# Hybrid attention and SSM layer: where 26 conditioning granules are summed, and in which order the middle stage loads

## The chip, the cores and the metric

The kernel runs on one core of a Trainium2 chip. The metric is the device time of one launch in microseconds (us). The engines are TensorE (PE, matrix multiply), VectorE (DVE), ScalarE (ACT), GpSimd (POOL) and SyncE (SP, which here issues the large transfers). The core has 16 DMA engines between HBM and the on-chip memory.

## The reference, cut to what matters

One decoder layer on 256 tokens of width 2048, all in float32. A vector `c` gives six vectors of 2048 numbers (shift, scale and gate of both sub-layers) through one large matrix, `w_ada`, of 2048 by 12288 (100 MB):

```python
c_act = jax.nn.silu(c)
ada = c_act @ w_ada[l] + b_ada[l]
sh_m, sc_m, gt_m, sh_f, sc_f, gt_f = [t[:, None, :] for t in jnp.split(ada, 6, axis=-1)]

h = rmsnorm(x, g_pre_mix[l]) * (1.0 + sc_m) + sh_m
proj = h @ w_in[l]                       # q (1024), k, v (128 each), u (1024)
attn = sliding_window_attention(q, k, v, attn_sinks[l])   # window 128, 16 heads
y = s5_ssm(u, ...)                       # 64 groups of 16 channels, 64 complex states each
z = gelu(y);  ssm = z * sigmoid(z @ w_glu[l])
merged = concat([rmsnorm(attn, g_attn_out[l]), rmsnorm(ssm, g_ssm_out[l])])
x = x + (1.0 + gt_m) * rmsnorm(merged @ w_out[l], g_post_mix[l])

h = rmsnorm(x, g_pre_ffn[l]) * (1.0 + sc_f) + sh_f
up = causal_depthwise_conv(h @ w_up[l], conv_w[l], conv_b[l])
ff = gelu(gate) * val @ w_down[l]
x = x + (1.0 + gt_f) * rmsnorm(ff, g_post_ffn[l])
```

## The kernel before, in words

**Granules.** Each of the six vectors is made in 16 granules of 128 numbers; a granule needs a block of `w_ada` of 1 MB. There are two ways. VectorE sums it (`ada_sum`, L142): one instruction multiplies the 128x2048 block by the broadcast `silu(c)` and adds along the row. Or PE does it (`ada_mm`, L155, 32 matmuls for a granule; ScalarE copies the result; `ada_cols`, L162, two small matmuls turn it into a column). `ON_PE` says which granules are PE's: ten of the first gate (GT_M), all of the FFN shift (SH_F), all of the first shift, four of the first scale (SC_M 0, 1, 11, 12). The rest of GT_M and the FFN scale SC_F, 22 granules, are the list `late_ada`: VectorE sums them in the middle stage, the GLU and the output projection.

**Stages in time.** Projection A (to about 160 us) makes q, k, v, u column by column; between its granules VectorE and GpSimd make Z, the complex tables of the SSM, in eight chunks (`z_chunk`). The middle stage (to 260 us) holds the rest of the input projection (`B(k4, kk)`, `mm_winb`, four loads `winb`), the attention of eight head pairs (`att_scores`, `att_max`, `att_norm`, `pv`, `att_out`) and the SSM: `k_half` makes kernel values in `kdz` and writes them out to a DRAM buffer `md`; `toeplitz` (L741) reads `md` back as the matrix `M` in four loads; `scan` runs 13 recurrence steps on VectorE; `y_mu` (L813) multiplies by `M`, `y_cx` (L826) by Z. Each group of four matmuls of `y_mu` uses two of `M`'s four loads, and its first eight groups use all four. Then GLU (`ps_g` L1039), the output projection (`wout` loads, split by `out_hl` into a high and a low part by ScalarE and VectorE, matmuls to `mix` at L566 and L557, to 385 us), the up projection (`ps_u` L1261, L1263), the down projection. In the first 16 tiles of the up projection, SH_F is made by PE in eight pairs (`shift_pair`, `shift_cols`).

**Order.** PE and SP run in the order in which the code is written, everywhere. In the middle stage VectorE, ScalarE and GpSimd do too: `in_order` (L72) records each of their instructions behind the one before, which is why their rows there show L72. So the code's order is the queue order, and an instruction that waits holds all behind it on its engine. All 1 MB loads (`raw`, L96) go through one pool of six buffers; a load waits until the buffer that it takes has been read. Which load is issued when is set by the list `loads` and by `pump(n)`, which takes the next n letters: w is a `winb`, d a granule that VectorE will sum, p one for a PE pair, g a part of `w_glu`. `do()` sums the oldest loaded d granule on VectorE and pumps one; `pair()` has PE multiply two p granules and pumps two; `cols()` finishes the oldest pair:

```python
def cols():
    res, part, o = pairs.pop(0)
    ada_cols(part, 2, res)
    A.copy(ada[:, o:o + 2], res)
```

In the output projection, step k loads `wout` ahead, calls `ld` once or twice (one `late_ada` load each), runs its matmuls and sums one or two granules.

## Time and profile before

| what | value |
|---|---|
| device time, median of 3 runs | 1172.07 us (1169.95 to 1172.98) |
| the profiled execution's own time | 1171.59 us |
| its span in the trace | 1169.8 us |
| mean granted TensorE clock | 0.987 of full speed |
| PE busy | 1126.6 us, 96% |
| VectorE busy | 873.7 us, 75% |
| ScalarE busy | 556.4 us, 48% |
| DMA | 325.87 MB, 279 GB/s on average |

Busy shares are averages over stages with different limits, so they don't say what a change in one stage is worth; that is read from the stage's own windows and waits. The program's time is 1.8 us more than the span.

### The profile page before, as it was taken

How to read it: one execution, taken by the hardware profiler on the slowest of the kernel's cores; microseconds unless marked ns; L12 is line 12 of the kernel's file. 1: busy time of each engine (PE TensorE's matmuls, PEld its weight loads, DVE VectorE, ACT ScalarE, POOL GpSimd, SP SyncE). 2: the span in 40 equal slices, each digit the busy share in tenths (PEclk: the TensorE clock that was granted, in tenths of full speed). 3: DMA queues.
4: the chain of work that ended last, by engine and by line, in shares of the span. 5: the costliest groups of instructions: out<-in, count | busy, mean ns of one | idle time of the engine just before them, and what ended most of it. 6: DMA issues, size and time to landing. Idle time of an engine off the chain costs nothing.

```text
span 1169.8 us, 18819 instructions
## 1 busy us (share of the span) xinstructions
PE 1126.6 (96%) x7504; PEld 944.9 (81%) x7504; DVE 873.7 (75%) x1369; ACT 556.4 (48%) x943; POOL 103.4 (9%) x96
## 2 busy tenths in 40 slices
PE   7899998989998999999999999999999999999996
PEld 5788876768786888888888888888888788888885
DVE  5987938636789787568999989886766776776555
ACT  3122143563534464446665665655555544444443
POOL 6005801024000200000000000000000000000002
PEclk9999998999998999999999999999999999999998
DMA  9899987787999469885787787865555777777712
GB/s 385 345 362 361 353 286 289 277 328 283 347 357 414 156 252 356 333 326 216 290 294 278 294 290 268 301 256 184 198 194 180 272 273 296 279 282 286 260 66 73
DMA packets 49144, 325.87 MB, mean 279 GB/s; under 512 B 5520, under 2 KB 7744, under 8 KB 12448
## 3 DMA queue, kind: packets, MB, share of 16 engines
q1 hardware_dynamic: 48240, 321.06, 73.6%
q0 software_dynamic: 672, 3.55, 0.8%
q8 instruction: 59, 0.97, 0.3%
q14 instruction: 29, 0.24, 0.1%
q10 hardware_dynamic: 144, 0.05, 0.0%
HBM read 317.27 MB, written 7.37 MB: 278 GB/s over the span
## 4 chain that ended last, share of the span: by engine, by line
PE 63%; issue 22%; DVE 8%; ACT 3%; DMA 2%; POOL 1%; DVEq 0%; ACTq 0%; POOLq 0%
PE ps_u L1261 27%; PE ps_u L1263 14%; PE accA L337 7%; PE ps_ada L155 4%; DVE l_wout L72 2%; PE ps_g L1039 2%; DVE ada L142 2%; PE accB L607 2%; DMA wout<-in_w_out_dram 1%; DVE scn L72 1%; PE ps_u L1250 1%; PE mix L557 1%; DMA shm<-in_w_ada_dram 1%; PE ps_wt L298 1%; PE ps_y L813 1%
## 5 line engine op out<-in xcount | busy, mean ns | idle before, releaser
L547 ACT CAST h_wup<-wup 128x1024 fp32r<-128x1024 f32 x168 | 176.5, 1052 | 194.6 <-PE ps_u L1261 175.6
L548 DVE TENSOR_TENSOR l_wup<-wup,h_wup 128x1024 fp32r<-128x1024 f32 x168 | 205.3, 1223 | 84.3 <-ACT h_wup L547 77.0
L1261 PE MATMUL ps_u<-h2B,h_wup 128*128 128x512 f32 x688 | 243.7, 395 | 0.0
L1261 PE MATMUL ps_u<-h2A,h_wup 128*128 128x512 f32 x688 | 243.5, 395 | 0.0
L1263 PE MATMUL ps_u<-h2A,l_wup 128*128 128x256 f32 x688 | 191.9, 279 | 0.0
L1263 PE MATMUL ps_u<-h2B,l_wup 128*128 128x256 f32 x688 | 191.5, 278 | 0.0
L548 DVE TENSOR_TENSOR l_wdn<-wdn,h_wdn 128x1024 fp32r<-128x1024 f32 x88 | 107.6, 1224 | 66.0 <-ACT h_wdn L547 65.9
L1261 PEld LDWEIGHTS ps_u<-h2B,h_wup 128*128 128x128 f32 x688 | 129.0, 188 | 30.3 <-issue 0.6
L1261 PEld LDWEIGHTS ps_u<-h2A,h_wup 128*128 128x128 f32 x688 | 128.9, 188 | 29.8 <-issue 0.4
L1263 PEld LDWEIGHTS ps_u<-h2A,l_wup 128*128 128x128 f32 x688 | 129.4, 188 | 0.8 <-issue 0.6
L547 ACT CAST h_wdn<-wdn 128x1024 fp32r<-128x1024 f32 x88 | 92.6, 1053 | 78.6 <-PE dn L566 70.4
L1263 PEld LDWEIGHTS ps_u<-h2B,l_wup 128*128 128x128 f32 x688 | 129.4, 188 | 0.2 <-issue 0.2
L337 PE MATMUL accA<-hT,win 128*128 128x256 f32 x448 | 109.6, 392 | 1.6 <-ACT hT L397 1.6
L566 PE MATMUL dn<-h_wdn,fl 128*128 128x512 f32 x336 | 105.0, 396 | 1.4 <-DVE fl L548 1.4
L566 PE MATMUL dn<-h_wdn,fh 128*128 128x512 f32 x336 | 106.0, 396 | 0.0
L566 PE MATMUL dn<-l_wdn,fh 128*128 128x512 f32 x336 | 106.0, 395 | 0.0
L337 PEld LDWEIGHTS accA<-hT,win 128*128 128x128 f32 x448 | 83.0, 194 | 14.7 <-issue 3.4
L142 DVE CUSTOM_DVE_ANT_0 ada<-ada,cbc 128x2048 f32<-128x2048 f32 x38 | 86.6, 2284 | 0.0
L566 PEld LDWEIGHTS dn<-h_wdn,fl 128*128 128x128 f32 x336 | 63.0, 188 | 17.1 <-DVE fl L548 1.9
L566 PEld LDWEIGHTS dn<-l_wdn,fh 128*128 128x128 f32 x336 | 63.1, 188 | 15.2
L566 PEld LDWEIGHTS dn<-h_wdn,fh 128*128 128x128 f32 x336 | 63.0, 188 | 15.2
L1417 DVE CUSTOM_DVE_ANT_0 wupt<-wupt,shbc 128x2048 f32<-128x2048 f32 x22 | 50.3, 2284 | 0.2 <-DMA wupt<-in_w_up_t_dram 0.2
(357 smaller groups left out, 1568.0 us busy)
## 6 DMA issues: line engine op xcount, KB each, us to landing
wup<-in_w_up_dram SPq DMA_DIRECT2D x88, 1024.0 KB
ada<-in_w_ada_dram SPq DMA_DIRECT2D x64, 1024.0 KB
wdn<-in_w_down_dram SPq DMA_DIRECT2D x44, 1024.0 KB
wupt<-in_w_up_t_dram SPq DMA_DIRECT2D x22, 1024.0 KB
scm<-in_w_ada_dram SPq DMA_DIRECT2D x16, 1024.0 KB
shm<-in_w_ada_dram SPq DMA_DIRECT2D x16, 1024.0 KB
wout<-in_w_out_dram SPq DMA_DIRECT2D x16, 1024.0 KB
win<-in_w_in_a_dram SPq DMA_DIRECT2D x16, 896.0 KB
```

What stands on the lines that cost most here:

```text
L72: self.last = self.no_earlier(getattr(self.e, name)(*args, **kw))
L142: return nc.vector.tensor_tensor_reduce(t, t, cbc, 1.0, 0.0, ALU.mult, ALU.add, accum_out=dst)
L155: PE.matmul(ps[32 * j:32 * j + 32, v * P:(v + 1) * P], lhsT=csil[:, kc:kc + 1].to_broadcast([P, 32]), rhs=t[:, kc * P:(kc + 1) * P], start ...
L337: PE.matmul(accA[ct // 2][:, (ct % 2) * S:(ct % 2 + 1) * S], lhsT=winA[k][:, ct * P:(ct + 1) * P], rhs=hk, start=(k == 0 and ct % 2 == 0), ...
L547: (A.copy if e[0] == "a" else V.tensor_copy)(hi, src)
L548: (V if e[1] == "v" else G).tensor_sub(lo, src, hi.bitcast(F32))
L566: PE.matmul(acc[tt * 4 + half * 2 + n2], lhsT=a_[:, tk], rhs=b_[:, n2 * 512:(n2 + 1) * 512], start=(kk == 0 and first), stop=(kk == nk - 1 ...
L607: PE.matmul(accB[ct // 2][:, (ct % 2) * S:(ct % 2 + 1) * S], lhsT=wt[:, kk * 512 + ct * P:kk * 512 + (ct + 1) * P], rhs=hT[k // 8][:, k % ...
L1039: PE.matmul(psg[ct][:, :S], lhsT=wg_[ct // 2][:, (ct % 2 * 8 + k) * P:(ct % 2 * 8 + k + 1) * P], rhs=zf[:, k], start=(k == 0), stop=(k == 7))
L1261: PE.matmul(ps, lhsT=wh[:, ks], rhs=h2[kk // 4][:, kk % 4].rearrange("p a b -> p (a b)"), start=(kk == 0), stop=(kk == KD - 1), skip_group ...
L1263: PE.matmul(ps[:, :S], lhsT=wl[:, ks], rhs=h2_of(kk)[0], start=False, stop=(kk == KD - 1), skip_group_check=True)
L1417: V.tensor_tensor_reduce(t, t, shbc[0], 1.0, 0.0, ALU.mult, ALU.add, accum_out=rlate[:, vg, f:f + 1])
```

## The change

The diff makes these edits. (1) Four granules of the FFN shift, SH_F 0 to 3, leave PE: `late_ada` grows from 22 to 26, and `shift_pair` runs for six pairs in place of eight; one small VectorE add puts the bias on the four columns. SC_M 10 is made on PE and SC_M 12 by VectorE. (2) VectorE makes six chunks of Z in place of five, GpSimd two in place of three, with its own scratch tile. (3) In the middle stage five sums by VectorE are added in front (`do()` twice, `do(0)` three times), the load list begins in another order and has 15 d in place of 10, and more of it is pumped ahead of `md` and of `M`. (4) `att_max(2)` and `att_norm(2)` come one and two scan steps earlier. (5) `cols()` copies its result on VectorE, not ScalarE, and `pv(5)`, `pv(6)` stand ahead of `z_part(0)`, `z_part(1)`. (6) The output projection loads and sums one granule fewer (11 in place of 12).

```diff
-Z_AT = (10, 11, 12, 13, 14)
-
-ON_PE = {(v, m) for v, n in ((SH_M, KD), (GT_M, 10), (SH_F, KD)) for m in range(n)} | {(SC_M, m) for m in (0, 1, 11, 12)}
+Z_AT = (10, 11, 12, 13, 14, 15)
+
+NSH = 4
+ON_PE = {(v, m) for v, n in ((SH_M, 0), (GT_M, 0), (SH_F, NSH)) for m in range(n, 10 if v == GT_M else KD)} | {(SC_M, m) for m in (0, 1, 10, 11)}
...
-    Z_AT_G = (10, 11, 12)
+    Z_AT_G = (10, 11)
...
-    late_ada = [(v, m) for v in (GT_M, SC_F) for m in range(KD) if (v, m) not in ON_PE]
+    late_ada = [(v, m) for v in (GT_M, SC_F, SH_F) for m in range(KD) if (v, m) not in ON_PE]
...
-    loads = "w w w w d p p d p p d p p d p p d p p d g d g d g d g d".split()
+    loads = "d d w d d w d w w d p p d p p d p p d p p d p p d g d g d g d g d".split()
...
             if n in Z_AT:
-                z_chunk(Z_AT.index(n), V, ztmp2)
+                z_chunk((0, 1, 2, 3, 6, 7)[Z_AT.index(n)], V, ztmp2)
...
-    def do():
+    def do(n=1):
         after[0].no_earlier(ada_sum(*ada_in.pop(0), cbc[0]))
-        pump()
+        pump(n)
...
         ada_cols(part, 2, res)
-        A.copy(ada[:, o:o + 2], res)
+        V.tensor_copy(ada[:, o:o + 2], res)
...
+    do()
     k_half(0)
+    do()
     att_scores(0)
     k_half(1)
     att_max(0)
+    do(0)
     v_tok()
...
     att_max(1)
+    do(0)
+    do(0)
     B(0, 2)
...
     B(0, 3)
-    pump()
+    pump(3)
...
     B(1, 1)
-    scan(2)
+    scan(1)
     att_max(2)
     att_out(1)
     B(1, 2, 3)
-    pump()
-    scan(2)
+    pump(2)
+    scan(1)
     att_norm(2)
     B(2, 0)
+    scan(2)
     pv(2)
...
     pair()
+    pv(5)
     z_part(0)
-    pv(5)
     cols()
...
-            ld(2 if k in (4, 6, 8) else 1)
+            ld(2 if k in (4, 6) else 1)
...
-        for _ in range(2 if k in (5, 7, 9) else 1):
+        for _ in range(2 if k in (5, 7) else 1):
...
+    V.tensor_add(shift[:, 1, :NSH], ada[:, SH_F * KD:SH_F * KD + NSH], col("bT")[:, SH_F * KD:SH_F * KD + NSH])
...
-                if n % 2 == 0 and n < KD:
-                    shp = shift_pair(n)
-                elif n < KD:
+                if n % 2 == 0 and n < KD - NSH:
+                    shp = shift_pair(NSH + n)
+                elif n < KD - NSH:
```

SP's queue around `md` and `M`, before (`winb` is a w load, `ada` a d load, `ud` and `U` carry u through DRAM):

```order
L619 DMA ud<-uT 128x8x128 x2
L637 DMA U<-ud 128x1024 x2
L664 DMA md<-kdz 8x16x1024 x8
L96 DMA ada_56_1565<-in_w_ada_dram 128x2048
L741 DMA M<-md 128x2048 x4
```

The same place now:

```order
L622 DMA ud<-uT 128x8x128 x2
L640 DMA U<-ud 128x1024 x2
L97 DMA ada_56_1332<-in_w_ada_dram 128x2048
L97 DMA winb_1371<-in_w_in_b_dram 128x2048
L667 DMA md<-kdz 8x16x1024 x8
L97 DMA winb_1575<-in_w_in_b_dram 128x2048
L97 DMA ada_59_1577<-in_w_ada_dram 128x2048
L97 DMA ada_60_1579<-in_w_ada_dram 128x2048
L744 DMA M<-md 128x2048 x4
```

One d and one w load now stand between `U` and `md`, and a w, a d and a p load between `md` and `M`, where one d load stood: four more loads ahead of `M`. The four others that stood ahead of `ud` changed their kind, not their number.

VectorE's queue where the sum stands that follows the second `cols()`, before (`zy` is a result of the SSM, `ast` a softmax's statistics, `s__2056` the scores of the seventh head pair):

```order
L72 COPY zy<-ps_y 128x4x8x16
L72 TENSOR_TENSOR ast<-ast 128x2x2
L72 RECIPROCAL ast<-ast 128x2x2
L142 ISA ada_60_1827,ada<-ada_60_1827,cbc 128x2048
L142 ISA ada 128x1
L72 ISA s__2056,ast<-ps_s,mask,c_71 128x128
L72 ISA ast 128x1
```

The same place now (`s__2072` are those scores):

```order
L73 COPY zy<-ps_y 128x4x8x16
L73 TENSOR_TENSOR ast<-ast 128x2x2
L73 RECIPROCAL ast<-ast 128x2x2
L73 COPY ada<-ps_ada 128x2
L143 ISA ada_65_1843,ada<-ada_65_1843,cbc 128x2048
L143 ISA ada 128x1
L73 ISA s__2072,ast<-ps_s,mask,c_71 128x128
L73 ISA ast 128x1
```

The copy of the pair's result, which waits for PE, now stands in front of the sum and of the seventh head pair's maxima; VectorE had nothing of the pairs in its queue before.

## Rows read from the trace of the kernel before

**Rows 1.** The page's part 4: the whole span's chain, shares by engine.

```profile
PE 63%; issue 22%; DVE 8%; ACT 3%; DMA 2%; POOL 1%; DVEq 0%; ACTq 0%; POOLq 0%
```

**Rows 2.** Window: us; PE, PEld, DVE, ACT, POOL busy; PEclk, DMA share, GB/s.

```profile
420.00:870.00 450.00, 450.00 (x2965) 392.37 (x2966) 369.53 (x601) 254.64 (x401) 1.08 (x2) 1.00 0.74 271
```

**Rows 3.** The chain of waits, 480 to 516: start us, us, what.

```profile
492.31 1.88 PE ps_ada L155 x64
...
498.16 0.34 PE ps_ada L162 x4
```

**Rows 4.** The chain of waits over the span: start us, us, what.

```profile
359.33 11.35 DMA wout<-in_w_out_dram
```

**Rows 5.** Timeline of PE at the output projection: start, us, what, idle before.

```profile
371.88 0.80 PE L557 MATMUL mix<-h_wout,mh 128*128 128x512 f32 x1 [3.06 <-ACT h_wout L72]
373.14 0.80 PE L557 MATMUL mix<-l_wout,mh 128*128 128x512 f32 x1 [0.46 <-DVE l_wout L72]
```

**Rows 6.** Window 371.7 to 378.5: columns as in Rows 2.

```profile
371.70:378.50 6.80, 6.16 (x14) 4.50 (x15) 6.59 (x8) 4.90 (x8) 0.00 (x0) 0.50 1.01 393
```

**Rows 7.** The page's part 5: the VectorE sum of one granule.

```profile
L142 DVE CUSTOM_DVE_ANT_0 ada<-ada,cbc 128x2048 f32<-128x2048 f32 x38 | 86.6, 2284 | 0.0
```

**Rows 8.** Timeline of DVE, 143 to 198.

```profile
143.31 0.68 DVE L270 TENSOR_TENSOR Z<-pwt,czd 128x512 f32<-128x512 f32 x1
...
153.77 0.69 DVE L72 COPY uT<-accA 128x512 f32<-128x512 f32 x1 [3.48 <-PE accA L337]
...
160.89 0.27 DVE L72 TENSOR_TENSOR kdz<-kdz,dd 128x64 f32<-128x64 f32 x1 [2.91 <-ACT kdz L72]
...
167.75 0.16 DVE L72 TENSOR_TENSOR ast<-ast 128x4 f32<-128x4 f32 x1 [2.30 <-ACT ast L72]
...
175.46 0.69 DVE L72 COPY W<-ps_v 128x512 f32<-128x512 f32 x1 [5.79 <-PE ps_v L677]
...
193.43 1.13 DVE L72 TENSOR_TENSOR scn<-Vs,scn 128x256 f32<-128x256 f32 x2
...
197.91 0.17 DVE L72 TENSOR_TENSOR ast<-ast 128x4 f32<-128x4 f32 x1
```

**Rows 9.** Timeline of PE in the middle stage, before the pairs.

```profile
198.86 1.78 PE L788 MATMUL ps_p<-c,s__1645 128*128 128x128 f32 x6 [5.57 <-ACT s__1645 L72]
...
211.38 2.05 PE L813 MATMUL ps_y<-M,U 128*32 128x128 f32 x32
...
216.91 0.82 PE L788 MATMUL ps_p<-c,s__1761 128*128 128x128 f32 x6
```

**Rows 10.** Timeline of SP's DMA issues, 168 to 194.

```profile
168.12 11.96 SPq L664 DMA_DIRECT2D md<-kdz  x8
180.19 1.17 SPq L96 DMA_DIRECT2D ada<-in_w_ada_dram  x1
193.73 1.91 SPq L741 DMA_DIRECT2D M<-md  x4
```

**Rows 11.** Three windows while md and M move: columns as in Rows 2.

```profile
172.00:181.00 9.00, 9.00 (x164) 7.64 (x163) 3.01 (x6) 1.82 (x8) 0.00 (x0) 0.90 0.51 197
181.00:187.00 6.00, 5.96 (x37) 4.54 (x35) 4.33 (x8) 3.73 (x9) 0.00 (x0) 1.00 0.75 300
196.00:206.00 10.00, 7.14 (x35) 4.78 (x35) 9.67 (x18) 2.49 (x7) 0.00 (x0) 0.66 1.01 424
```

**Rows 12.** Timeline of PE at the fourth softmax and third pair.

```profile
234.71 0.61 PE L162 MATMUL ps_ada<-sel,parts 128*128 128x1 f32 x4
...
241.15 1.95 PE L155 MATMUL ps_ada<-ada,csil 128*32 128x128 f32 x64 [0.75 <-ACT qT L72]
```

**Rows 13.** Timeline of DVE, the sum after the second pair's columns.

```profile
230.94 2.29 DVE L142 CUSTOM_DVE_ANT_0 ada<-ada,cbc 128x2048 f32<-128x2048 f32 x1
...
234.63 0.17 DVE L72 TENSOR_SCALAR ast<-ast 128x4 f32<-128x4 f32 x1
```

**Rows 14.** Timeline of ACT between them.

```profile
237.23 0.40 ACT L72 ACTIVATE s__2056<-s__2056,ast 128x128 f32<-128x128 f32 x1
```

More of the change, by code (lines that the diff above doesn't have):

```diff
@@ L311, in decoder_layer @@
     c_in = czd[:, 0:1024].rearrange("p (a b c) -> p a b c", a=2, b=NQ)
-    ztmp = czd[:, 1152:1664].rearrange("p (a b c) -> p a b c", a=QN, b=T)
     ld_win(1)
@@ L315, in decoder_layer, with z_chunk @@
     Z = []
-    def z_chunk(qc, e=G, ztmp=ztmp):
+    def z_chunk(qc, e, ztmp):
         if qc == 0:
@@ L524, in decoder_layer @@
             if n in Z_AT:
-                z_chunk(Z_AT.index(n), V, ztmp2)
+                z_chunk((0, 1, 2, 3, 6, 7)[Z_AT.index(n)], V, ztmp2)
             if n in Z_AT_G:
-                z_chunk(len(Z_AT) + Z_AT_G.index(n))
+                if n == Z_AT_G[0]:
+                    ztmpg = act.tile([P, QN, T, SH], F32, tag="B0", name="ztmpg")
+                z_chunk(4 + Z_AT_G.index(n), G, ztmpg)
             if n == KD - 1:
@@ L989, in decoder_layer @@
     pair()
+    pv(6)
     z_part(1)
-    pv(6)
     cols()
@@ L1441, in decoder_layer @@
                     norm_h2(n - 2)
-                if n % 2 == 0 and n < KD:
-                    shp = shift_pair(n)
-                elif n < KD:
+                if n % 2 == 0 and n < KD - NSH:
+                    shp = shift_pair(NSH + n)
+                elif n < KD - NSH:
                     shift_cols(*shp)
-                    if n == KD - 1:
+                    if n == KD - NSH - 1:
                         ps = bank(6, "ps_row")
```

## The prediction

> **What bounds the kernel now.** I read the chain of waits by engine first: PE holds 63% of it and another 22% is issue, in which no other engine is waited for, so in most stages PE itself sets the end [rows 1]. A window over most of the up projection says it plainly: PE is busy for 450.00 of 450 us at full clock [rows 2]. There the reader is to see that whatever leaves PE shortens the run by its whole length, and that work put on VectorE there, busy for 370 of 450, is free. Next I read PE's timeline for the places where PE does wait, since only there can a move of other engines' work count: 5.57 us ahead of the third softmax's transposes at 198.86 [rows 9], 3.06 and 0.46 us at the end of the output projection [rows 5]. Last come the transfers around `M`, in SP's timeline [rows 10] and by windows [rows 11], because the change puts loads there. The profiled execution took 1171.59 us, 0.5 under the median of 1172.07; the sum below is made against it.
>
> **Part 1, the FFN shift leaves PE by four granules: -4.4 us.** In the chain a pair costs 1.88 us for 64 matmuls at L155 and 0.34 us for the four small ones at L162 [rows 3], 2.22 us, and two of eight pairs go: 4.4 us, all of it on the path since PE never waits there [rows 2]. Bounds -4 (a load that now comes sooner wins nothing) and -5 (the matmul behind each pair starts more smoothly). The four columns are ready long before, and the small VectorE add that they need lies in the output projection's tail, some 0.17 us, as an addition of 128x4 takes at 197.91 [rows 8].
>
> **Part 2, the output projection has one load and one sum fewer: -4.5 us.** The chain there runs through 11.35 us of waiting for a `wout` transfer [rows 4], and the DMA share is still 1.01 in the window behind it, at 393 GB/s [rows 6]; then PE waits 3.06 us for the high half and 0.46 for the low half of a late `wout` [rows 5]. A load of 1 MB at the 424 GB/s that this core reaches [rows 11] is 2.5 us, a sum on VectorE 2.28 us [rows 7]. So the last `wout` blocks are some 2.4 us earlier, and of the 3.5 us of waiting about 1.1 is left. [...] That is 2.4 and 2.1: -4.5. Bounds: -7 (all of wait and clock) and 0 (another transfer or the low half is late in its place).
>
> **Part 3, five sums in the front of the middle stage: 0.** Each is 2.28 us [rows 7]. VectorE idles 2.91 us ahead of the first `kdz` addition and much the same ahead of the second, 2.30 us ahead of the first softmax's normalising, and 5.79 us ahead of the copies of `ps_v` at 175.46 [rows 8]. One sum goes into each of the first three gaps and two into the last. That is the cover; if a load is late there, the copies are late by as much, up to 2 us.
>
> **Part 4, the softmax moved up: it only lengthens another wait.** Between the maxima of the third softmax and its normalising stand two scan steps, from 193.43 to 197.91, 2.24 us each [rows 8]. Now the maxima come one step sooner and the normalising two: near 193.6, 4.3 us earlier. PE's 5.57 us of waiting [rows 9] falls to about 1.2, and the low clock behind it, 0.66 on average in 196 to 206 and so 3.4 us lost [rows 11], most likely goes too. PE then comes to `y_mu(0)`, at 211.38 before [rows 9], between 203.5 and 207. What is late next is `M`.
>
> **Part 5, four more loads ahead of `M`: +6.5 us.** The writes of `md` leave half of the DMA engines unused: 0.51 of the engines' time at 197 GB/s [rows 11]. A load issued beside them at 180.19 [rows 10] lifts the rate to 300 GB/s for 6 us [rows 11]: 103 GB/s times 6 is 0.62 MB, so a good half of its 1 MB went through on the free engines, and the rest had to follow the writes on the others. `M` was issued at 193.73 [rows 10] and its 4 MB moved by 206 at 424 GB/s [rows 11]. On the half that carries `md`, each further load adds half its bytes on half the engines, the same 2.5 us as on all. Four more make 9.9 us: `M` complete near 215.9. The first groups of `y_mu(0)` can run from about 211, the last ones end near 216.9, where they ended at 213.4 [rows 9]: +3.5 us at full clock. But PE has waited for some 4 to 7 us by then, as long as the waits behind which the clock fell [rows 5, 6, 9, 11], and the 3.5 us of `B` up to the next softmax at 216.91 [rows 9] would take up to 7. I take 3 for the clock. Bounds: 0 (`M` is in time) and +10 (the clock falls twice).
>
> [...]
>
> **Part 6, the pairs' results copied by VectorE: +2.2 us.** VectorE's copy waits for PE's small matmuls of 234.71, done at 235.3 [rows 12]; behind it in its queue stand a sum of 2.29 and the next maxima, 1.6 us from 233.2 to 234.8 [rows 13]. The maxima end at 239.2, and ScalarE's exponentials, begun at 237.23 before [rows 14], come 2 us later; the copy of `qT` and with it the third pair at 241.15 (which waited 0.75) [rows 12] follow. `pv(5)` ahead of `z_part(0)` gives about as much back at the next softmax as the following copy takes again. Bounds 0 and +4.5.
>
> **Part 7, one chunk of Z more on VectorE: +0.7 us.** Six operations of 0.68 us [rows 8] are 4.1 us in a gap of 3.48 us ahead of the copies of `uT` [rows 8]: 0.6, and a little for SC_M 12 on VectorE. Bounds 0 and 2.
>
> **Sum.** -4.4 - 4.5 + 0 + 6.5 + 2.2 + 0.7 = +0.5 us: 1172.1 against 1171.59. A measurement of this kernel can't tell less than 0.3%, 3.5 us, from no change.
>
> **The rivals.** A: `M` isn't late. If the added loads run through on the engines that `md` leaves free, there is room: half of some 420 GB/s over 172 to 196 is 5 MB, just the five loads there. `M` then lands by 208, PE wins its earlier softmax, part 5 is 0 or a little less, and with part 6 at half and part 7 the middle is +1: -4.4 - 4.5 + 1 = -7.9, 1163.7. Against it stands the load of 180.19, of which only half went that way.
>
> B, slower: `M` is late and the clock falls again with every wait that follows. From 9.9 us of delay on, PE waits in `y_mu(0)` twice (for the second load of `M` and for the last), runs `B` at half speed (+10), and the waits of 2 us at the third pair and the columns bring another low stretch (+3.4 on part 6). Part 2 stands at -3 then: -4.4 - 3 + 10 + 3.5 + 0.7 = +6.8, 1178.4. It decides as soon as part 5 is above +9. For it: half clock behind both long waits of before. Against: two low stretches so close to each other, with PE at work between them, stand in no row.
>
> C: the output projection gives nothing, since another transfer, or the low half behind the sums on VectorE, is late in its place: +0.5 + 4.5, 1176.6. For it: VectorE and DMA are both nearly full there [rows 6].
>
> **How the numbers follow.** Forecast 0.50, own range 1167 to 1177, of which 0.38 lies within 0.3%, 0.07 below and 0.05 above. A 0.24, all faster. B 0.16 and C 0.10, all slower. Faster 0.31, same 0.38, slower 0.31. Range: from A's middle, 1163.5, to B's, 1178.5, which leaves about 0.2 outside.
>
> **What would show it.** In the changed profile: L155's pairs in the up projection six in number; at `y_mu(0)` a PE wait that ends with `M`'s transfer, of 4 us or more, and a granted clock near 0.5 behind it (A: no such wait); no wait above 2 us at the third softmax; a VectorE copy that waits for `ps_ada` ahead of the sums; at the end of the output projection a PE wait of about 1 us (C: 3 or more). I am wrong if `M`'s last load lands before 210, or if the middle stage ends earlier than before.

## The result and the profile after

The changed kernel takes 1178.41 us, the median of 5 runs (1176.01 to 1185.81), against 1172.07 us before: ratio 1.0058, 95% interval 1.003 to 1.0086. It is slower by about 6 us. The profiled execution took 1177.27 us, with a span of 1175.5 against 1169.8. Of that difference of 5.7 us each stage has its own part. The table takes the start of the same matmul in both traces; the last two columns are what the stretch before it gained or lost by itself.

| start of | before, us | after, us | later by | own part | forecast |
|---|---|---|---|---|---|
| first attention scores | 159.64 | 156.93 | -2.7 | -2.7 | +0.7 (part 7) |
| fourth softmax on PE | 216.91 | 219.64 | +2.7 | +5.4 | +6.5 (parts 3 to 5) |
| first matmul of the output projection | 291.3 | 301.4 | +10.1 | +7.4 | +2.2 (part 6) |
| first matmul of the up projection | 392.3 | 396.3 | +4.0 | -6.1 | -4.5 (part 2) |
| first matmul of the down projection | 911.8 | 917.7 | +5.8 | +1.8 | -4.4 (part 1) |
| end of the span | 1169.8 | 1175.5 | +5.7 | -0.1 | |

The stage of which the forecast was surest, the up projection, is the one that came out with the wrong sign. The page of the changed kernel begins with the span; its part 4 answers to [rows 1], and its part 5 has the large matmul of the up projection (busy us, mean ns of one, idle before):

```profile
span 1175.5 us, 18554 instructions
...
PE 75%; DVE 9%; issue 7%; DMA 5%; ACT 3%; POOL 1%; SPq 0%; DVEq 0%; ACTq 0%; POOLq 0%
...
L1271 PE MATMUL ps_u<-h2B,h_wup 128*128 128x512 f32 x688 | 247.1, 398 | 0.0
```

The same row of the page before:

```profile
L1261 PE MATMUL ps_u<-h2B,h_wup 128*128 128x512 f32 x688 | 243.7, 395 | 0.0
```

As many matmuls of one shape, none of which waits, take longer. Two windows of the up projection, free of the FFN shift's pairs, before (columns as in [rows 2]):

```profile
600.00:770.00 170.00, 170.00 (x983) 148.65 (x982) 154.51 (x244) 101.94 (x163) 0.00 (x0) 1.00 0.78 286
785.00:900.00 115.00, 115.00 (x666) 100.56 (x665) 79.29 (x114) 63.13 (x95) 0.00 (x0) 1.00 0.55 192
```

And after:

```profile
600.00:770.00 170.00, 170.00 (x965) 147.37 (x964) 151.61 (x238) 100.56 (x161) 0.00 (x0) 1.00 0.77 280
785.00:900.00 115.00, 115.00 (x653) 99.76 (x652) 77.53 (x111) 62.08 (x92) 0.00 (x0) 1.00 0.54 186
```

The reader is to see that busy time and granted clock say "PE is full" in all four, while the count of matmuls in the same time is 1.8 to 2.0% lower after. Busy 100% is no measure of progress here. The timeline shows it at the single matmul. Before (start, us, what; the eighth large matmul begins 2.43 us behind the first):

```profile
699.68 0.39 PE L1261 MATMUL ps_u<-h2B,h_wup 128*128 128x512 f32 x1
...
702.11 0.40 PE L1261 MATMUL ps_u<-h2A,h_wup 128*128 128x512 f32 x1
```

After, the same stretch (2.48 us):

```profile
699.66 0.40 PE L1271 MATMUL ps_u<-h2A,h_wup 128*128 128x512 f32 x1
...
702.14 0.40 PE L1271 MATMUL ps_u<-h2B,h_wup 128*128 128x512 f32 x1
```

Over longer stretches a pair of one large (512 columns) and one small matmul (256) takes 346.7 ns before and 353.3 ns after; this regular distance is called the cadence below. Sixteen such pairs make one tile of the result. Before, 346.7 holds on average from the 22nd of the 86 tiles to the last; after, nearly all tiles run at 353.3. The starts of the tiles part the stage in two: up to the 22nd tile the changed kernel gained 5.0 us (153.9 us from the stage's start, against 158.9), about what part 1 said; from there to the down projection it lost 6.8 (367.5 against 360.7), some 64 tiles of 16 pairs by 6.6 ns. The trace of before has both cadences in it: its 16th to 20th tile run at 353.3 as well.

In the middle stage PE's timeline after, with its idle times in brackets, answers to [rows 9, 12]:

```profile
192.81 1.53 PE L791 MATMUL ps_p<-c,s__1655 128*128 128x128 f32 x6 [1.08 <-ACT s__1655 L73]
...
205.30 0.63 PE L816 MATMUL ps_y<-M,U 128*32 128x128 f32 x4 [2.00 <-DMA M<-md]
207.80 0.66 PE L816 MATMUL ps_y<-M,U 128*32 128x128 f32 x4 [1.86 <-DMA M<-md]
210.28 0.66 PE L816 MATMUL ps_y<-M,U 128*32 128x128 f32 x4 [1.83 <-DMA M<-md]
212.76 1.59 PE L816 MATMUL ps_y<-M,U 128*32 128x128 f32 x20 [1.83 <-DMA M<-md]
214.28 5.52 PE L610 MATMUL accB<-hT,winb 128*128 128x256 f32 x16
219.64 0.82 PE L791 MATMUL ps_p<-c,s__1777 128*128 128x128 f32 x6
...
246.05 3.21 PE L156 MATMUL ps_ada<-ada,csil 128*32 128x128 f32 x64 [2.91 <-ACT qT L73]
...
266.05 1.01 PE L163 MATMUL ps_ada<-sel,parts 128*128 128x1 f32 x4 [2.42 <-ACT parts L73]
```

The third softmax waits 1.08 us in place of 5.57, and PE then waits four times for `M`, 7.5 us in all. Each of the three places with long waits (`M`, the pair at 246.05, the columns at 266.05) has a stretch at half clock, 0.52 of full speed over each of these windows (PEclk is the third number from the right, ahead of DMA share and GB/s):

```profile
207.40:217.70 10.30, 6.25 (x36) 4.04 (x37) 5.04 (x16) 4.91 (x16) 0.00 (x0) 0.52 0.91 363
245.10:248.60 3.50, 2.55 (x48) 2.37 (x52) 0.00 (x0) 0.90 (x3) 0.00 (x0) 0.52 0.02 5
265.50:272.40 6.90, 6.36 (x22) 5.53 (x23) 2.70 (x3) 1.58 (x4) 5.32 (x5) 0.52 1.02 406
```

SP's issues after, which answer to [rows 10]: the writes of `md`, then what stands between them and `M`.

```profile
166.36 11.82 SPq L667 DMA_DIRECT2D md<-kdz  x8
178.28 4.28 SPq L97 DMA_DIRECT2D winb<-in_w_in_b_dram  x1
182.66 2.24 SPq L97 DMA_DIRECT2D ada<-in_w_ada_dram  x2
195.56 1.91 SPq L744 DMA_DIRECT2D M<-md  x4
```

How the copies by VectorE reach the third pair: VectorE's timeline after, in answer to [rows 13],

```profile
238.16 0.16 DVE L73 COPY ada<-ps_ada 128x2 f32<-128x2 f32 x1 [4.43 <-PE ps_ada L163]
238.24 2.29 DVE L143 CUSTOM_DVE_ANT_0 ada<-ada,cbc 128x2048 f32<-128x2048 f32 x1
...
241.92 0.17 DVE L73 TENSOR_SCALAR ast<-ast 128x4 f32<-128x4 f32 x1
```

and ScalarE's, in answer to [rows 14]:

```profile
242.13 0.40 ACT L73 ACTIVATE s__2072<-s__2072,ast 128x128 f32<-128x128 f32 x1 [2.05 <-DVE ast L73]
...
245.65 0.35 ACT L73 COPY qT<-ps_o 128x256 f32<-128x256 f32 x1
```

The copy waits 4.43 us for PE with the sum and the maxima behind it, so ScalarE's exponentials begin at 242.13, and the copy of `qT` for which the pair of 246.05 waits comes last.

At the end of the output projection one wait is left where [rows 5] had 3.06 and 0.46 us,

```profile
379.57 0.50 PE L560 MATMUL mix<-l_wout,mh 128*128 128x512 f32 x1 [0.90 <-DVE l_wout L73]
```

and the window around it is at full clock, where [rows 6] had 0.50:

```profile
372.00:380.00 8.00, 7.10 (x32) 5.58 (x31) 8.00 (x8) 4.54 (x6) 0.00 (x0) 1.00 1.05 412
```

### The profile page after: what moved, and what is told of

The parts are those of the page before. It is cut to its first block, busy times and chain, and to the rows that moved or that the text cites. A ratio compares the mean times of both kernels' runs of the same rounds, so it can differ in the third digit from the quotient of the medians.

```text
span 1175.5 us, 18554 instructions
## 1 busy us (share of the span) xinstructions
PE 1129.8 (96%) x7368; PEld 944.5 (80%) x7368; DVE 880.6 (75%) x1387; ACT 555.4 (47%) x936; POOL 94.6 (8%) x90
## 4 chain that ended last, share of the span: by engine, by line
PE 75%; DVE 9%; issue 7%; DMA 5%; ACT 3%; POOL 1%; SPq 0%; DVEq 0%; ACTq 0%; POOLq 0%
PE ps_u L1271 27%; PE dn L569 15%; PE ps_u L1273 14%; PE accA L337 7%; PE ps_ada L156 3%; DVE ada L143 3%; DVE l_wout L73 2%; PE ps_g L1048 2%; DMA md<-kdz 2%; DMA M<-md 1%; DMA winb<-in_w_in_b_dram 1%; PE ps_u L1260 1%; DMA shm<-in_w_ada_dram 1%; PE ps_wt L299 1%; PE accB L610 1%
## 5 line engine op out<-in xcount | busy, mean ns | idle before, releaser
L1271 PE MATMUL ps_u<-h2B,h_wup 128*128 128x512 f32 x688 | 247.1, 398 | 0.0
L1271 PE MATMUL ps_u<-h2A,h_wup 128*128 128x512 f32 x688 | 246.7, 398 | 0.0
L143 DVE CUSTOM_DVE_ANT_0 ada<-ada,cbc 128x2048 f32<-128x2048 f32 x42 | 96.4, 2298 | 6.2 <-DMA ada<-in_w_ada_dram 6.2
```

Source lines behind the costliest of these rows:

```text
L143: return nc.vector.tensor_tensor_reduce(t, t, cbc, 1.0, 0.0, ALU.mult, ALU.add, accum_out=dst)
L1271: PE.matmul(ps, lhsT=wh[:, ks], rhs=h2[kk // 4][:, kk % 4].rearrange("p a b -> p (a b)"), start=(kk == 0), stop=(kk == KD - 1), skip_group ...
```

## The experiments

The theory after the result: three separate losses outweigh the gains. They are the cadence of the up projection's pairs (about 6 us), `M` late behind the loads and the low clock behind it (5 to 7), and the copies by VectorE with their two low stretches (7). The rival for the cadence is that it is only chance of one traced execution; for `M`, that the half-used engines of [rows 11] hold it back; for the copies, that the wait for `qT` is hidden by something else in the end. Medians of the kernel before were 1170.6 to 1171.8 us beside these runs; the ratios below are against it. They differ a little from the quotients of the medians (for e6 0.9877 against 0.990).

**e1_cols_scalar: the changed kernel, pairs' columns copied by ScalarE again.**

```diff
-        V.tensor_copy(ada[:, o:o + 2], res)
+        A.copy(ada[:, o:o + 2], res)
```

> The changed kernel with one edit undone: the pairs' results are copied by ScalarE again. Theory: from the fourth softmax (pv(3)) to the first output-projection matmul the changed kernel lost 7.4 us against before, because VectorE's copy waits for PE ahead of a 2.3 us sum; so the 2.9 us wait at the third pair and the 2.4 us wait at the last columns go, with the low clock behind them, and the GLU starts 5 to 7 us earlier. Of that the output projection, which is bound by transfers, keeps 2 to 5 us: up projection's start -2 to -5. Rival: the late M alone moves everything, and the copies' engine is indifferent: under 1 us at the GLU's start. The up projection's cadence (353 or 347 ns for a large and a small matmul) may fall either way and is worth 6 us; I read it apart.

Measured: 1171.83 us, ratio 0.9995 (0.9978 to 1.0012). PE's timeline at the third pair in its trace, and the window behind it:

```profile
243.83 1.95 PE L156 MATMUL ps_ada<-ada,csil 128*32 128x128 f32 x64 [0.76 <-ACT qT L73]
```

```profile
245.00:272.00 27.00, 23.90 (x338) 19.47 (x328) 7.37 (x16) 15.65 (x40) 9.21 (x11) 1.00 0.88 351
```

The wait is back at 0.76 and the clock stays full in this trace. The first matmul of the output projection comes 1.7 us later than before in place of 10.1, though the fourth softmax is as late as after (219.6). So the copies cost 8.4 us there, and 6.6 by the medians. That is the high end: from the fourth softmax to the output projection the other pairs of traces that differ in the copies alone give 4.0 (e4 against e2), 4.1 (e5 against e3) and 8.0 (e6 against e10). Over all traces this stretch takes 79.0 to 82.5 us with VectorE's copies (seven) and 73.4 to 77.5 with ScalarE's (nine). The full clock is not ScalarE's doing alone: with its copies, e4, e5, e7, e8, e9 and e11 have one or two stretches of 3.4 us at half clock there. The up projection starts 8.0 us sooner than after, more than expected, and ran at 353.3 ns.

**e2_md16: the changed kernel, `md` written so that all sixteen engines carry it.**

```diff
-            for n in range(T):
-                nc.sync.dma_start(md[n].rearrange("h g x -> g h x"), kdz[:, n * SH * T:n * SH * T + P * T])
+            for g in range(8):
+                src = kdz[g * SH:(g + 1) * SH, :P * T]
+                nc.sync.dma_start(md[:, :, g].rearrange("t h x -> h t x"),
+                                  dap(src, 0, [src.ap[0], [SH * T, T], [1, P * T]]))
```

> The changed kernel with md written in another cut: eight writes of 16 partitions by 8 rows each (16x8x1024) in place of 8x16x1024, the same bytes to the same places; loads and order as they are. Theory: the old cut uses half of the DMA engines, and that is why M, with four more loads ahead of it, is late. With all 16, the 4 MB of md take some 10 us and not 21, M lands near 202 to 206, and the four waits of 1.8 to 2.0 us in y_mu(0) and the low clock behind them go: the fourth softmax 5 us earlier. Rival: the writes are limited by something else (HBM writes, one issuer): the rate stays near 200 GB/s while md moves, and M lands near 213 as it does.

Measured: 1181.49 us, ratio 1.009 (1.0073 to 1.0107), a miss. Its window over the writes, and the last wait for `M` in PE's timeline:

```profile
178.00:188.00 10.00, 9.85 (x65) 7.88 (x64) 7.95 (x18) 4.33 (x10) 0.00 (x0) 1.00 1.00 220
```

```profile
218.22 1.58 PE L818 MATMUL ps_y<-M,U 128*32 128x128 f32 x20 [2.50 <-DMA M<-md]
```

All sixteen engines are busy (share 1.00 against 0.51 in [rows 11]), yet they move 220 GB/s where half of them moved 197. The number of engines wasn't what held the writes, as the rival had it. `M` ended 5.5 us later than after, not sooner; that the loads now had no idle half of the engines to go through fits this, but no run shows it by itself. What limits the writes stays open.

**e4_both** (e1 and e2 together).

> The changed kernel with both the copies on ScalarE and md in the cut 16x8x1024. Theory: both losses of the middle stage go, the GLU starts 8 to 12 us earlier than in the changed kernel and thus about 1 to 4 us earlier than in the kernel before; the up projection starts 4 to 8 us earlier. With the fast cadence 1162 to 1167, with the slow one 6 us more. Rival: the output projection's transfers take the gain back, and the up projection starts at 398 or later.

Measured: 1171.23 us, ratio 1.0001 (0.9978 to 1.0024), a miss. In its trace the fourth softmax is at 222.3, worse than after, as in e2 (224.3), and the up projection starts 3.3 us sooner than after, but it took the 347 ns cadence from the 23rd tile by itself. So the cadence isn't a fixed property of the changed code.

**e3_nudge: the changed kernel, one small matmul in the middle of the 29th tile issued ahead of its large one.** The work is the same (the expectation counts this tile as the 30th); two small ones and then two large ones come to stand in a row. Such rows of two stand in the 21st to 26th tile of the kernels before and after as well, where three small matmuls run later than their places in the code.

```diff
+                if (f, vg, kk) == (15, 0, 8):
+                    hi_lo.reverse()
```

> The changed kernel with two neighbouring matmuls of the up projection exchanged once, in tile 30 of 86 (the small one ahead of the large one at one of 16 places): the same work and sums. Theory: the 6.3 us that the up projection lost against before come from a cadence of PE (353.4 ns for each large and small matmul where before had 346.7) that persists until something disturbs it, so one exchange can switch it: if it switches, the run is 5 to 6 us faster, at the latest from that tile on, and if not, the time is the same within 1 us; either way both cadences are the only two levels to be seen. Rival: the slower cadence is caused by what else runs (transfers, VectorE, ScalarE), and then one exchange can't change it for longer than a tile.

Measured: 1172.54 us, ratio 1.001 (0.9992 to 1.0027), 5.9 us under the changed kernel. Its trace begins the up projection at the same 396.3 us, runs at 353.3 ns up to the exchange at 592.7 and at 346.7 from there to the end, and starts the down projection at 911.7, 6.0 sooner than after:

```profile
600.00:770.00 170.00, 170.00 (x983) 149.91 (x982) 154.44 (x243) 102.06 (x163) 0.00 (x0) 1.00 0.78 286
```

The count is that of before, 983. So there are two steady cadences of the same instructions at the same clock, and one exchange led from the slower to the faster. None led back: in e10, and at the later place in e11, it met the faster cadence and left it so.

**e12_late_swap, e13_swap_beat9, e14_swap_beat10: the same exchange 32 tiles later, at the ninth, tenth and eleventh pair of the tile.** If the time follows the tiles behind the switch, half of e3's gain is left. In the 353 ns cadence the starts of large matmuls are 361, 349 and 350 ns apart in turn, a beat of three, so three pairs in a row try all phases.

```diff
-                if (f, vg, kk) == (15, 0, 8):
+                if (f, vg, kk) == (31, 0, 8):
```

(9 and 10 in place of the last number, 8, in e13 and e14.)

> The changed kernel with the one exchange at tile 60 in place of tile 28. Theory: the slow cadence lasts until the exchange, wherever that stands: 353.3 ns up to tile 60, 346.7 behind it, 25 tiles of 16 pairs at 6.6 ns, 2.7 us faster than the changed kernel (about 1175.5), half of what the early exchange brought. Rival: the early exchange helped through something else near 597 us: no switch here.

> The changed kernel with the exchange in tile 60, one pair of matmuls later (place 9 of 16 in place of 8). Theory: the slow cadence is a repeat of three pairs (361, 349, 350 ns), and which of them the exchange meets decides. In tile 28 it met the pair behind a 361 and switched; 512 pairs later, two over a multiple of three, place 8 met another and didn't; place 9 meets the same one as in tile 28: 353.3 ns up to tile 60, 346.7 behind it, 2.7 us faster than without. Rival: late exchanges don't switch, or it is chance: 353.3 ns to the end.

> The same, two pairs later (place 10). Theory: this meets the third pair of the repeat, of which no exchange has shown the outcome; by the three-pair repeat it is one fixed outcome, fast or slow from tile 60 on, and no level between 346.7 and 353.3 ns. Rival: another level, or a switch elsewhere than at tile 60.

Measured: e12 1178.87 us, ratio 1.006 (1.0031 to 1.0089), no switch, a miss; e13 1174.54, ratio 1.0025 (1.0004 to 1.0045), switched; e14 1178.76, ratio 1.0053 (1.0028 to 1.0077), no switch. e13's two windows, on either side of its exchange at 773:

```profile
600.00:770.00 170.00, 170.00 (x964) 147.45 (x963) 151.54 (x239) 100.80 (x162) 0.00 (x0) 1.00 0.77 280
785.00:900.00 115.00, 115.00 (x665) 101.43 (x664) 79.94 (x115) 62.61 (x94) 0.00 (x0) 1.00 0.54 189
```

and e12's second:

```profile
785.00:900.00 115.00, 115.00 (x653) 99.75 (x652) 78.29 (x117) 62.63 (x94) 0.00 (x0) 1.00 0.56 196
```

e13 goes from 964, a count of the slower cadence (965 after), to 665, one of the faster (666 before); e12 stays at 653. No switch, a late one and an early one give ratios of 1.006, 1.0025 and 1.001, in the order of the tiles behind the switch, but e13's interval overlaps those of its neighbours. The record parts them better. It has the span and the mean granted clock of every execution, with a trace or without; their product is an estimate of the span at full clock, without what the half clock cost:

| kernel | executions | span times clock, us |
|---|---|---|
| changed | 5 | 1157.4 to 1161.5, median 1159.0 |
| e12 and e14, no switch in their traces | 18 | 1157.2 to 1161.5 in 15, 1152.0 to 1153.1 in 3 |
| e4, faster cadence in its trace | 12 | 1149.9 to 1151.7 in 5, 1156.3 to 1159.7 in 7 |
| e13, late switch | 12 | 1152.8 to 1157.4, median 1156.5 |
| e3, early switch | 11 | 1150.4 to 1157.6, median 1154.2 |
| before, beside all these runs | 91 | 1152.2 to 1157.8 in 77, 1160.0 to 1163.2 in 14 |

By the medians a late switch is worth 2.5 us and an early one 4.8, where the traces' 6.6 ns for each pair make 2.7 and 6.0. Before and e4 show two groups some 6 us apart among the executions of one and the same kernel. So the changed kernel mostly stands where the slower cadence would put it, and the kernel before does so in about one execution of seven. That the groups are the two cadences in executions without a trace too is argued from their distance, not shown.

Which pair of the beat the exchange meets decides whether it switches: in all seven traces in which it met the slower cadence at the place of e3 in the beat (e3, e5, e6, e7, e9, e13 and the first exchange of e11) it switched, at the two other places (e12 and e14, one trace each) it didn't.

**e7_before_nudge: the kernel before with e3's exchange.**

> The kernel before with the same one exchange of two matmuls in the up projection. Theory of a cadence that the last disturbance leaves behind: it was fast here (346.7 ns from tile 25 on), so the exchange leaves it fast (time the same, 1170 to 1173) or makes it slow (6 us more, 1176 to 1179); a time between those would speak against two levels. Rival (the changed kernel is slow in the up projection for what else it runs): no change.

Measured: 1171.5 us, ratio 0.9988 (0.9961 to 1.0015), no difference. In its trace the seven tiles ahead of the exchange ran at 352 ns on average, which in the trace of before ran at 347 with the same instructions, and from the exchange on it ran at 346.7: the cadence varies between executions of the same code, and the exchange switched it here too.

**e8_before_ffn: the kernel before with the four FFN granules summed in the output projection, and no other edit.** Four more loads and sums stand there.

```diff
-            ld(2 if k in (4, 6, 8) else 1)
+            ld(2 if k in range(4, 11) else 1)
...
-        for _ in range(2 if k in (5, 7, 9) else 1):
+        for _ in range(2 if k in range(5, 12) else 1):
```

> The kernel before with only the FFN part: four shift granules leave PE, and VectorE sums them in the output projection with four more loads there (16 in place of 12); middle stage and projection A as before. Theory: the up projection's pairs give 4.4 us, but the output projection is bound by transfers, and each load more there costs 2.5 us: its end 8 to 10 us later, in all 1174 to 1178 at the fast cadence. Rival: the transfers there hide: 1167 to 1169.

Measured: 1184.66 us, ratio 1.0086 (1.0052 to 1.012). From the first matmul of the output projection to the first of the up projection it took 10.7 us more than before, 2.7 for each load with the clock that went with it. PE's longest waits there (us in total, times, longest):

```profile
PE mix L567 <- ACT h_wout L73: 3.4, 1, 3.4
PE mix L558 <- ACT hl_wout L73: 2.8, 1, 2.8
PE mix L558 <- DVE hl_wout L73: 2.6, 1, 2.6
```

With them the clock fell twice, where [rows 6] had one such stretch of 6.8 us. The second is

```profile
379.00:389.20 10.20, 5.23 (x11) 3.33 (x12) 10.17 (x13) 5.95 (x8) 0.00 (x0) 0.50 0.92 356
```

Its 10.2 us at half clock cost at most 5.1 of the 10.7, so a load by itself costs 1.4 to 2.7 us. That is the price of part 2, seen from the other side. Its up projection ran at 353 ns; less the 6.8 us between the two cadences it would be near 1178, the upper end of what was expected.

**e5_cols_nudge** (e1's and e3's edits), **e6_m_earlier** (e5, and two of the three loads issued behind `M`), **e10_m_cols_vector** (e6 without e1's edit). The edit of e6:

```diff
     B(0, 3)
-    pump(3)
+    pump(1)
...
     toeplitz()
+    pump(2)
```

> The changed kernel with the pairs' copies on ScalarE and, in the up projection, the one exchange of two matmuls. Theory: the two gains add up, since they lie in stages that do not touch: up projection's start near 388 as with the copies alone, and if the cadence is 346.7 ns, 1164 to 1166, some 6 us faster than the kernel before. Rival: the cadence depends on when the up projection starts, so the same exchange falls into the slow one here: 1170 to 1172.

> As the last one, and of the three loads between the writes of md and the loads of M two (a granule for VectorE, one for a pair) are issued behind M. Theory: each of them holds M up by its own 2.5 us, so M's last load lands near 208 and not 213, the waits in y_mu(0) shrink from some 7 to 2 to 4 us, and the fourth softmax (pv(3)) comes 3 to 5 us earlier; of that the output projection, bound by transfers, keeps a part: 0 to 3 us at the up projection. Rival: M is late because the writes of md are slow, whatever is queued; then pv(3) stays at 219 to 220.

> The changed kernel with the one exchange and two of the loads behind M, but the pairs' copies on VectorE as the change has them. Theory: the late M and the copies' engine are two separate losses: pv(3) near 214.5 as in the kernel with both edits, then some 5 us lost up to the GLU's start, of which the output projection takes most back (its transfers are bound): up projection's start 385 to 390. Rival: with M in time the waits behind VectorE's copies are absorbed: GLU start as with ScalarE's copies, within 1 us of 256.6.

Measured: e5 1167.06 us, ratio 0.9943 (0.992 to 0.9966); e6 1160.16, ratio 0.9877 (0.9844 to 0.991); e10 1166.82, ratio 0.9961 (0.9948 to 0.9975). PE in e6's trace:

```profile
203.83 0.64 PE L816 MATMUL ps_y<-M,U 128*32 128x128 f32 x4 [1.72 <-DMA M<-md]
...
208.79 1.59 PE L816 MATMUL ps_y<-M,U 128*32 128x128 f32 x20 [1.83 <-DMA M<-md]
...
214.48 0.82 PE L791 MATMUL ps_p<-c,s__1777 128*128 128x128 f32 x6
```

With two loads fewer ahead of it the last part of `M` comes 4 us sooner, and the fourth softmax 5.2. Counted from the first attention scores, PE's last wait for `M` ends after 55.8 us in the changed kernel and 50.9 in e6, 2.5 us for each load. Over all traces the fourth softmax comes 61.8 to 63.0 us behind those scores with the three loads ahead of `M` (seven, without e2 and e4) and 56.6 to 58.6 with one (four). The losses are separate: by the medians the copies cost 5.5 (e5 against e3) or 6.7 (e6 against e10), `M` 6.9 (e6 against e5) or 5.7 (e10 against e3), the cadence 5.9. e5 stayed a little above its forecast (up projection's start at 391.1, not 388), and e6 gained more than its own: the up projection starts 7.9 us sooner than in e5, where 0 to 3 was expected; between the first attention scores and that start its trace has 6.8 us of half clock and e5's 20.5. e6 is the best version found, 1.2% faster than the kernel before (0.9 to 1.6).

**e11_two_swaps** (e6 with a second exchange, 15 tiles sooner) and **e9_pool_tmp** (e6 with GpSimd's scratch tile back in `czd`, as before).

```diff
-                if (f, vg, kk) == (15, 0, 8):
+                if (f, vg, kk) in ((7, 1, 8), (15, 0, 8)):
```

```diff
-                z_chunk(4 + Z_AT_G.index(n), G, ztmpg)
+                z_chunk(4 + Z_AT_G.index(n), G, czd[:, 1152:1664].rearrange("p (a b c) -> p a b c", a=QN, b=T))
```

> The fastest kernel so far with a second exchange of the same kind in tile 13 of the up projection, where the slow cadence begins. Theory: it switches there too, tiles 13 to 20 run at 346.7 ns for each pair of matmuls: 8 tiles of 16 pairs at 6.6 ns, 0.8 us, and up to 0.8 more in tiles 21 to 27; 0 to 2 us faster, hard to tell in the times, plain in the trace. Rival: an exchange can lead from a cadence to itself, nothing changes in tiles 13 to 27.

> The fastest kernel so far (copies on ScalarE, two loads behind M, one exchange) with GpSimd's scratch for Z back in the tile that it had before. Theory: projection A is 1.9 us shorter in the changed kernel because GpSimd's second and third operation on Z do not run near 29 us any more, beside small VectorE operations that then took 1.04 and 1.21 us where they take 0.18 without; with the old scratch they run there again, and the first attention scores come 1.5 to 2.5 us later (157.9 to about 159.8). Rival: the gain comes from the other number of Z chunks: no change.

Measured: e11 1161.67 us, ratio 0.9913 (0.9891 to 0.9935); its tiles behind the second exchange did switch, but the interval overlaps e6's. e9 1162.38, ratio 0.992 (0.9897 to 0.9943), not told apart from e6 either. e9 has the same number of chunks as e6 and the old scratch, and its trace shows the place where projection A gained. VectorE in e9:

```profile
29.38 1.04 DVE L440 TENSOR_TENSOR t<-t 128x32 f32<-128x32 f32 x1
...
30.56 1.21 DVE L442 TENSOR_TENSOR t<-t 128x32 f32<-128x32 f32 x1
```

and GpSimd in e9:

```profile
29.26 1.12 POOL L272 TENSOR_TENSOR czd<-pwt,czd 128x512 f32<-128x512 f32 x1
30.45 1.27 POOL L273 TENSOR_TENSOR Z<-Z,czd 128x512 f32<-128x512 f32 x1
```

The first of these VectorE instructions in the changed kernel, where no GpSimd instruction runs beside it:

```profile
29.09 0.18 DVE L440 TENSOR_TENSOR t<-t 128x32 f32<-128x32 f32 x1
```

Beside a GpSimd instruction the two take 1.04 and 1.21 us, as in the kernel before, and 0.18 and 0.19 in the changed kernel: about a microsecond more each. What that did to PE stands in PE's timelines, before and after:

```profile
33.74 1.93 PE L155 MATMUL ps_ada<-shm,csil 128*32 128x128 f32 x32 [2.92 <-DVE shift L395]
```

```profile
32.44 1.08 PE L156 MATMUL ps_ada<-shm,csil 128*32 128x128 f32 x32 [1.71 <-DMA shm<-in_w_ada_dram]
```

Before, PE waited 2.92 us for a result of VectorE that comes behind these additions, and the 32 matmuls behind the wait took 1.93 us in place of 1.08, at half clock (0.50 from 33.8 to 37.2); after, the wait ends with a transfer after 1.71, at full clock. The matmuls after that come 2.9 us sooner than before (38.63 and 35.72), so this place holds the whole gain of the two traces. e9 gave back less than forecast: its attention scores come at 158.9, those of e6 at 157.9. They scatter, 159.4 to 160.0 in the three traces with the kernel before's projection A (before, e7, e8) and 156.7 to 158.8 in eleven of the twelve with the changed one; the twelfth, e12, has one more stretch of half clock, from 143.2, and 160.8. By the medians the gain is 1.9 us.

## Why the prediction was right or wrong

**Part 1 is the step that failed.** Its term was right by itself: six pairs in place of eight, and 5.0 us gained up to the 22nd tile, for a forecast of 4.4. What failed is the step that carried it to the end, that the reader sees PE busy for all of a window and that whatever leaves PE there "shortens the run by its whole length". PE at 100% and full clock has two speeds on these pairs, 346.7 and 353.3 ns, and the trace of before stood in the faster one from the 22nd tile on. The changed kernel stands in the slower one and loses 6.8 us there, more than the pairs gave, so that the stage came out at +1.8 in place of -4.4. e3 and e13, which switched, and e12 and e14, which didn't, show that it is this, and that one exchange can take it away. Nothing in the trace of before warned of it but one thing that I didn't look at: whether the distance of two matmuls is the same all through the stage; it is 353.3 in the 16th to 20th tile and 346.7 behind the 26th. All traces but e11's stand at 353.3 in the 16th to 20th tile, and they part in the 21st to 26th. Why the changed program mostly comes out of them in the slower beat is not shown; e4 and e7 say that it isn't fixed by the code, and the spans times clock, that the kernel before isn't always in the faster one.

**Part 6 had the mechanism and the wrong size**: +7.4 in place of +2.2. Up to the third pair it went as worked out: exponentials at 242.13, of which 2.7 us came from earlier and 2.2 from here. What the term left out is what the longer wait does: 2.91 us at 246.05 and 2.42 at 266.05 come with half clock (0.52 over 3.5 and 6.9 us), which by itself costs some 5.0 us (0.48 of 10.4, an estimate), about what the term was short of. That was written down under rival B, "the waits of 2 us at the third pair and the columns bring another low stretch", but hung on part 5 being above +9. It needed no such condition. e1 shows the first wait back at 0.76, the second gone and the clock full, with one line. By the length of this stretch the other traces with VectorE's copies lie 4.6 to 8.1 us above before's.

That rival B's time, 1178.4, is the measured median is luck. It had part 1 at -4.4 (measured +1.8) and part 5 at +10 (+5.4 with parts 3 and 4), and its sum has 3.5 for part 6, where its own words, 2.2 and 3.4 on top, make 5.6.

**Part 5 held**, +5.4 for +6.5, though its two halves were both off: the last wait for `M` ended at 212.76, not 215.9, and the low clock took `B` from 3.5 us to 5.52. The forecast had `M` late by the full 9.9 us of four loads, 206 to 215.9; the trace has it late by about 7 (212.76). The two of them that e6 took away cost 2.5 us each, as forecast; what the other two, ahead of `md`, cost no run shows. That half of each load has to follow the writes on their engines was an estimate from [rows 11]; no trace shows the order on a single engine. That `md`'s rate is low because only half of the engines carry it, the theory of e2, fell there: 220 GB/s at a share of 1.00, 197 at 0.51. Rival A, that `M` isn't late, fell with the four waits, and e6 shows what it would have been worth.

**Part 4 was right**: 1.08 us of waiting for a forecast of 1.2, and `M` next.

**Part 3 was right** but for one wait of PE, 0.7 us, on VectorE's copy of `W`, inside the +5.4: the sum ahead of it waited for its load, as part 3 had allowed.

**Part 2 was too small**: -6.1 for -4.5. The wait at the end is 0.90 us for a forecast of 1.1. The 2.1 us that the sum has for the clock no run shows: behind the wait the clock stayed full (1.00 from 372 to 380), where [rows 6] had 0.50 over 6.8 us, at most 3.4 us by estimate, so that nearly all of these came back; the other 2.7 us are then the load, at the upper end of e8's 1.4 to 2.7. The later start of the stage has no part in it: in the thirteen traces with this part it starts between 287.9 and 306.1, and takes 94.8 to 95.7 us in twelve of them (97.5 in e3, whose clock fell once) against 101.0 before. Rival C fell.

**Part 7 had the wrong sign**, -2.7 for +0.7: with a scratch tile of its own GpSimd no longer runs beside VectorE's small instructions near 29 us. That is the scratch and not the number of chunks, since e9 brings it back with the scratch alone. The six operations of the added chunk were counted, what GpSimd did to others was not.

The errors of the parts, -3.4 (7), -1.1 (3 to 5), +5.2 (6), -1.6 (2), +6.2 (1) and -0.1, come to +5.2: from +0.5 to +5.7 in the two traces; the medians are 6.3 us apart.

## What to carry to other kernels

Where one engine is busy all the time, look not only at its busy share and clock but at the distance of two equal instructions early and late in the stage: a stage of 500 us gained or lost 6 us by a rhythm that no wait shows. Count a wait on PE with the half clock that can follow it, for waits of two to three microseconds too (0.52 over 3.5 us with a wait of 2.91, over 6.9 with one of 2.42), before saying that a move of small work to another engine is cheap. Move a load behind the transfer that is late (2.5 us for each of two in e6), and try each of several edits alone: here gains and three losses came in one diff, and parting them made a kernel that is 1.2% faster than before.

## What the runs showed of the hardware that was not expected

- Large and small matmul pairs at full clock with PE 100% busy have two steady cadences, 346.7 and 353.3 ns. Each lasts for tens of tiles; a displaced matmul switches the slower to the faster or leaves it, by the pair of the three-beat that it meets (e3, e5, e6, e7, e9, e11 and e13 switched, e12 and e14 not).
- The writes of `md` move 197 GB/s at a DMA share of 0.51 and 220 at 1.00, while the window of `M`'s loads reaches 424 (e2, [rows 11]).
- Two VectorE instructions of 128x32, L440 and L442, take 0.18 and 0.19 us with no GpSimd instruction beside them (changed kernel), and 1.04 and 1.21 beside GpSimd instructions of 1.12 and 1.27 us (e9).
- The four waits for `M`, of 1.83 to 2.00 us each with some 0.6 us of work between them, came with the half clock (0.52 from 207.4 to 217.7), as the wait of 3.06 us in [rows 5, 6] did (0.50); the single wait of 0.90 us at 379.57 did not (1.00).
